# Dividing the merged attention heads earlier, in another loop, and handing them on through DRAM in token order

## The chip, the cores and the metric

The kernel runs on one core of a Trainium2 chip. The metric is the device time of one execution, in microseconds (us). TensorE (PE) multiplies matrices into PSUM; VectorE (DVE), ScalarE (ACT) and GpSimd (POOL) work on tiles in SBUF (DVE and ACT on PSUM too); SP, ACT and POOL also issue DMA transfers. Each engine has its own list of instructions, and they meet at semaphores.

## The reference

One layer of a decoder is computed for a prompt of 1024 tokens and 8 sample tokens with the same weights (1032 columns in all, `T`). The part that matters here:

```
h    = rms_norm(x, g_mix_pre)
q, k, v, c_b, u, g_a, g_c = project(h, w_in)
attn = merged heads of three dilated attention groups      # [1024, 512]: numerator / denominator
a    = attn @ w_attn_o                                     # 512 -> 1024
c    = (c_b * causal_conv(u)) @ w_conv_o                   # 1024 -> 1024
mix  = (sigmoid(g_a) * a + sigmoid(g_c) * c) @ w_o
x    = x + rms_norm(mix, g_mix_post)
x    = x + rms_norm(square(relu(rms_norm(x, g_ffn_pre) @ w_ff1)) @ w_ff2, g_ffn_post)
```

## The kernel before

All activations lie with channels on the 128 partitions and tokens along the row. The 1032 columns are taken in three chunks of 344 (`CH`). Every product is made of three matmuls, since each operand is split into a high part (a cast, `wh`, `hh`, `ah`) and the rest (a subtraction, `wl`, `hl`, `al`): high by high (L165), rest by high (L168), high by rest (L169). Weights come as tiles of 128x512 (`wr`), are split by ACT (L134) and by DVE or POOL (L135), and are held in at most seven pairs of buffers in the stages told of here.

`unit` computes one 128-row block of one projection for one chunk: 24 matmuls where the inner size is 1024, 12 where it is 512, all into one PSUM bank `ps_mm`. `bank` hands out four banks in turn, so a fifth chunk can begin only when the first has been read by whoever evacuates it.

The stages in question, in order:

- **Attention** writes, for each head, the unnormalised output `od_sum` to `num_d` in DRAM (L641) and the denominators to `den_d`. Within a row the tokens do not lie in order: they lie by class, that is by their remainder modulo 4, 256 tokens to a class. After it, the reciprocals of the denominators go to `rden_d` (L703), in the same order.
- **The convolution's projections**, which end with `cvh` and `cvl`.
- **The convolution's output projection** (`wco`, L933 to L951): for each of 8 row blocks `i`, three chunks of 24 matmuls on `cvh` and `cvl`; DVE multiplies each chunk out of PSUM with the sigmoid gate `sg[c]` into `m2` (L948; the tile is called m in the rows). For `i` under 4 the gate is loaded by POOL from `gc_d` (`gr`, L940) and ACT takes its sigmoid (L941); for the others PE computes the gate first. POOL stores each `m2` to `m2_d` (L950).
- **The attention output projection** (`wao`, L955 to L1015). When `cvh` and `cvl` are free, SP loads the numerators and the reciprocals, chunk by chunk and two of the four 128-row groups at a time, 86 tokens of a class at once (L972, L974): 36 transfers. Meanwhile PE computes the first attention gate (`g`, 72 matmuls). For each of six pieces DVE or POOL multiplies numerator by reciprocal (L981), and ACT and DVE split the product into `ah` and `al`, reading by class and writing in token order (L986, L987). Then PE alternates between two half units of the next gate and one chunk of the output projection: `run(ga, 2)`, `run(pa, 1)`, so 24 and 12 matmuls in turn.

Instructions that the code does not pin are placed on each engine by a scheduler, so the order on an engine is not always that of the lines. PE's order is that of the code.

Of the kernel before, what the change touches and what calls it, by code (L numbers as in the profile page):

```python
# [10 lines left out]
F32 = mybir.dt.float32  # L11
F32R = mybir.dt.float32r
AF = mybir.ActivationFunctionType
OP = mybir.AluOpType
# [4 lines left out]
P = 128  # L19
KT = 8  # L20
NQ = 1024
NB = 8
T = NQ + NB
CH = T // 3
# [3 lines left out]
def chunk(c):  # L28
    return slice(c * CH, (c + 1) * CH)
# [6 lines left out]
def tile_decoder_layer(  # L36
# [5 lines left out]
    nc = tc.nc  # L42

    const = ctx.enter_context(tc.tile_pool(name="const", bufs=1))
    dram = ctx.enter_context(tc.tile_pool(name="dram", bufs=1, space=DRAM))
# [16 lines left out]

    asm = const.tile([P, 4, NB], F32, name="asm")
    num_d = dram.tile([P, 4, NQ], F32, name="num_d")
    den_d = dram.tile([8, NQ], F32, name="den_d")
    rden_d = dram.tile([8, NQ], F32, name="rden_d")
    sq_d = dram.tile([NB, 3, 512], F32, name="sq_d")
# [103 lines left out]
    def whole(hi, lo):  # L171
        return lambda k, c: (hi[:, k, chunk(c)], lo[:, k, chunk(c)])
# [17 lines left out]
    def project(src, rhs, use):  # L190
        yield from several([(src, use)], rhs)
# [8 lines left out]
    def run(g, n=None):  # L200

        while n is None or n > 0:
            if next(g, run) is run:
                return
            n = n and n - 1
# [30 lines left out]
    def spread(ri):  # L236
        rb = bank(at, [P, 512], "ps_rb")
        for b, (o, w) in enumerate(NB3):
            pe(nc.tensor.transpose(rb[:, o:o + w], ri[:, b:b + 1].to_broadcast([P, P]), ident))  # L239
        return rb  # L240
# [37 lines left out]
    def copy_piece(n=1):  # L278
        for _ in range(n):
            if pieces:  # L280
                tc.keep_in_program_order(nc.scalar.dma_start(*pieces.pop(0)))


    with ExitStack() as st:
# [71 lines left out]
        with tc.tile_pool(name="xin", bufs=1) as xin:  # L356
# [26 lines left out]
            def apply(c, rb):  # L383
                return norm_apply(xin, x_sb[c], rb, 0, lambda k: hh[:, k:k + 2, chunk(c)],
                                  lambda k: hl[:, k:k + 2, chunk(c)],
                                  (nc.vector, nc.gpsimd) if c else (nc.vector,))
# [29 lines left out]
            a = apply(0, spread(ri))  # L416
# [11 lines left out]
            for c in range(3):  # L428
                run(g, 4)
                if c < 2:  # L430
                    ri = factors(sq)
                    run(g, 1)
                    a = apply(c + 1, spread(ri))
# [493 lines left out]
    def gate(pool, src, store):  # L927
        def use(c, ps):
            s = pool.tile([P, CH], F32, name="sg", tag="sg", bufs=4)
            nc.scalar.activation(s, ps, AF.Sigmoid)  # L930
            store[c] = s
        return project(src, h_in, use)

    lo_eng[:] = [nc.vector]
    with tc.tile_pool(name="sgc", bufs=1, side="right") as sgp:
        for i in range(KT):
            sg = {}
            if i < NRAW:
                gr = sgp.tile([P, T], F32, name="gr", tag="gr", bufs=2)
                nc.gpsimd.dma_start(gr, gc_d[i])  # L940
                nc.scalar.activation(gr, gr, AF.Sigmoid)  # L941
                sg = {c: gr[:, chunk(c)] for c in range(3)}
            else:
                run(gate(sgp, ("win", W1 + i), sg))
            m2 = sgp.tile([P, T], F32, name="m2", bufs=2)

            def use_cc(c, ps):
                nc.vector.tensor_tensor(m2[:, chunk(c)], ps, sg[c], op=OP.mult)  # L948
            run(project(("wco", i), whole(ch_, cl_), use_cc))
            nc.gpsimd.dma_start(m2_d[i], m2)  # L950
            copy_piece(1)  # L951
# [3 lines left out]
    with tc.tile_pool(name="apool", bufs=1) as apool:  # L955
        ah = apool.tile([P, 4, T], F32R, name="ah")
        al = apool.tile([P, 4, T], F32R, name="al")
        rv = rden_d.rearrange("(k a) t -> a k t", a=2)
        sgs = [{} for _ in range(KT)]
        with tc.tile_pool(name="pre", bufs=1) as pre:  # L960
            def by_class(t):
                return t.rearrange("p k (r j) -> p k r j", r=4)

            nums = []
            for c in range(3):
                w = min(NQ, CH * (c + 1)) - CH * c
                js = slice(CH // 4 * c, CH // 4 * c + w // 4)
                for k in (0, 2):
                    ks = slice(k, k + 2)
                    ar, rd = (pre.tile([P, 2, CH], F32, name=nm, bufs=6) for nm in ("num", "rden"))  # L970
                    for k1 in range(2):
                        nc.sync.dma_start(by_class(ar[:, :, 0:w])[:, k1], by_class(num_d[:, ks, :])[:, k1, :, js])  # L972
                        for a in range(2):
                            nc.sync.dma_start(by_class(rd[64 * a:64 * a + 64, :, 0:w])[:, k1],  # L974
                                              by_class(rv[a:a + 1, ks, :])[:, k1, :, js].to_broadcast([64, 4, w // 4]))
                    nums.append((c, ks, w, ar, rd))
            g = gate(apool, ("win", W1 + 8), sgs[0])
            for c, ks, w, ar, rd in nums:
                run(g, 1)
                s = slice(CH * c, CH * c + w)  # L980
                (nc.gpsimd if c else nc.vector).tensor_tensor(ar[:, :, 0:w], ar[:, :, 0:w], rd[:, :, 0:w], op=OP.mult)  # L981
                for k1 in range(2):
                    k = ks.start + k1
                    src = ar[:, k1, 0:w].rearrange("p (r j) -> p j r", r=4)
                    hi = ah[:, k, s].rearrange("p (j r) -> p j r", r=4)
                    nc.scalar.copy(hi, src)  # L986
                    nc.vector.tensor_tensor(al[:, k, s].rearrange("p (j r) -> p j r", r=4), src, hi.bitcast(F32),  # L987
                                            op=OP.subtract)
            nc.scalar.copy(ah[:, :, NQ:], asm)
            nc.vector.tensor_tensor(al[:, :, NQ:], asm, ah[:, :, NQ:].bitcast(F32), op=OP.subtract)  # L990
            run(g)
        mpool = m_stack.enter_context(tc.tile_pool(name="mpool", bufs=1, side="right"))
        mh = mpool.tile([P, KT, T], F32R, name="mh")
        ml = mpool.tile([P, KT, T], F32R, name="ml")

        def m2_tile():
            return apool.tile([P, CH], F32, name="m2c", tag="m2c", bufs=3)

        for i in range(KT):
            sg = sgs[i]  # L1000

            def use_a(c, ps):
                s = chunk(c)
                m2 = m2_tile()
                nc.gpsimd.dma_start(m2, m2_d[i, :, s])
                nc.vector.tensor_tensor(sg[c], ps, sg[c], op=OP.mult)
                nc.gpsimd.tensor_tensor(m2, m2, sg[c], op=OP.add)
                nc.scalar.copy(mh[:, i, s], m2)
                nc.vector.tensor_tensor(ml[:, i, s], m2, mh[:, i, s].bitcast(F32), op=OP.subtract)
            ga = gate(apool, ("win", W1 + 9 + i), sgs[i + 1]) if i + 1 < KT else iter(())  # L1010
            pa = project(("wao", i), whole(ah, al), use_a)
            for c in range(3):
                run(ga, 2)
                run(pa, 1)
            run(pa)  # L1015
            copy_piece(1)
# [320 lines left out]
```

## Time and profile before

| | us |
|---|---|
| median of 3 runs | 2048.09 (2047.76 to 2049.38) |
| the profiled execution's own time | 2052.08 |
| its span, first to last instruction | 2050.3 |
| PE busy with matmuls in the span | 1995.0 |
| DVE busy | 1056.0 |
| ACT busy | 687.2 |
| POOL busy | 512.7 |

The profile is of one execution, with the times of single instructions counted from the start of its span. PE is busy nearly all the time and its mean granted clock was 0.987 of full speed; so a gain can only come from a stretch in which PE waits or runs at a lower clock, and a loss from a new one.

### The profile page before, as it was taken

The numbers are of one execution on the slowest core, as the hardware profiler recorded it, in microseconds if no ns is written. First come the engines' busy times: TensorE is split into PE (matmuls) and PEld (weight loads), VectorE is DVE, ScalarE is ACT, GpSimd is POOL, SyncE is SP. The second block draws the span as 40 slices with busy tenths as digits, with TensorE's granted clock in tenths as the row PEclk, the third lists the DMA queues.
The fourth block names the chain that finished last, engine by engine and source line by source line (L and its number), as shares of the span: only waits on it lengthen the run. The fifth ranks groups of instructions, "written<-read, shape, count | busy, mean of one in ns | idle before, by whom it ended". The sixth has DMA issues, their size and how long they took to land. (4 is left out here: it accounts for less than half of the span.)

```text
span 2050.3 us, 31900 instructions
## 1 busy us (share of the span) xinstructions
PE 1995.0 (97%) x12877; PEld 1975.1 (96%) x12877; DVE 1056.0 (52%) x1829; ACT 687.2 (34%) x1351; POOL 512.7 (25%) x414
## 2 busy tenths in 40 slices
PE   7999999999999999999989999999999999999997
PEld 6999999999999999999989999899999999999996
DVE  7688668677653454642223321925554444444446
ACT  4365435544443222222113232543322222222233
POOL 3233413332333532520013232311211111111113
PEclk7999999999999999999999999999999999999998
DMA  4121222222324744435374441322221111111112
GB/s 145 53 71 38 87 68 66 58 87 89 107 67 151 227 160 162 156 134 198 114 169 130 140 155 33 96 93 84 98 88 43 52 45 49 42 47 57 42 32 83
DMA packets 89669, 195.52 MB, mean 95 GB/s; under 512 B 23489, under 2 KB 33857, under 8 KB 88625
## 3 DMA queue, kind: packets, MB, share of 16 engines
q1 hardware_dynamic: 78144, 116.97, 18.2%
q10 hardware_dynamic: 6672, 63.49, 9.3%
q0 software_dynamic: 4704, 13.01, 2.0%
q8 instruction: 101, 1.65, 0.3%
q14 instruction: 48, 0.39, 0.1%
HBM read 173.60 MB, written 74.29 MB: 121 GB/s over the span
## 5 line engine op out<-in xcount | busy, mean ns | idle before, releaser
L165 PE MATMUL ps_mm<-hh,wh 128*128 128x344 f32 x1824 | 594.2, 326 | 4.1 <-ACT sg L930 2.1
L168 PE MATMUL ps_mm<-hl,wh 128*128 128x344 f32 x1824 | 586.9, 322 | 3.7 <-DVE hl L248 1.9
L169 PE MATMUL ps_mm<-hh,wl 128*128 128x344 f32 x1824 | 586.3, 321 | 0.0
L135 POOL TENSOR_TENSOR wl<-wr,wh 128x512 fp32r<-128x512 f32 x177 | 235.4, 1331 | 867.5 <-ACT wh L134 827.2
L134 ACT CAST wh<-wr 128x512 fp32r<-128x512 f32 x320 | 195.3, 619 | 574.2 <-PE ps_mm L168 474.2
L165 PEld LDWEIGHTS ps_mm<-hh,wh 128*128 128x128 f32 x1824 | 346.6, 190 | 6.8 <-ACT hh L254 2.9
L168 PEld LDWEIGHTS ps_mm<-hl,wh 128*128 128x128 f32 x1824 | 346.1, 190 | 6.0 <-DVE hl L248 3.2
L169 PEld LDWEIGHTS ps_mm<-hh,wl 128*128 128x128 f32 x1824 | 346.1, 190 | 0.0
L165 PE MATMUL ps_mm<-gh,wh 128*128 128x344 f32 x768 | 246.2, 321 | 0.0
L165 PE MATMUL ps_mm<-rh,wh 128*128 128x344 f32 x768 | 245.9, 320 | 0.0
L169 PE MATMUL ps_mm<-rh,wl 128*128 128x344 f32 x768 | 245.8, 320 | 0.0
L169 PE MATMUL ps_mm<-gh,wl 128*128 128x344 f32 x768 | 245.4, 320 | 0.0
L168 PE MATMUL ps_mm<-gl,wh 128*128 128x344 f32 x768 | 245.4, 319 | 0.0
L168 PE MATMUL ps_mm<-rl,wh 128*128 128x344 f32 x768 | 245.0, 319 | 0.0
L1174 DVE TENSOR_TENSOR f<-ps_mm,f 128x344 f32<-128x344 f32 x336 | 167.2, 513 | 96.5 <-PE ps_mm L169 96.3
L1112 DVE TENSOR_TENSOR r<-r 128x344 f32<-128x344 f32 x96 | 59.6, 620 | 216.1 <-ACT rh L1111 216.0
L135 DVE TENSOR_TENSOR wl<-wr,wh 128x512 fp32r<-128x512 f32 x143 | 99.3, 698 | 128.2 <-ACT wh L134 128.0
L169 PEld LDWEIGHTS ps_mm<-gh,wl 128*128 128x128 f32 x768 | 144.7, 188 | 0.0
L168 PEld LDWEIGHTS ps_mm<-gl,wh 128*128 128x128 f32 x768 | 144.7, 188 | 0.0
L165 PEld LDWEIGHTS ps_mm<-gh,wh 128*128 128x128 f32 x768 | 144.7, 188 | 0.0
L165 PEld LDWEIGHTS ps_mm<-rh,wh 128*128 128x128 f32 x768 | 144.3, 188 | 0.0
L168 PEld LDWEIGHTS ps_mm<-rl,wh 128*128 128x128 f32 x768 | 144.3, 188 | 0.0
(255 smaller groups left out, 2935.2 us busy)
## 6 DMA issues: line engine op xcount, KB each, us to landing
wr<-in_win_dram SPq DMA_DIRECT2D x152, 256.0 KB, 2.9
wr<-in_wf_dram SPq DMA_DIRECT2D x128, 256.0 KB, 2.8
out_okv_dram<-in_cache_dram ACTq DMA_DIRECT2D x16, 1020.0 KB, 8.1
kt<-in_cache_dram SPq DMA_DIRECT2D x32, 256.0 KB, 3.4
x_sb<-in_xT_dram SPq DMA_DIRECT2D x12, 344.0 KB, 5.5
m_d<-m POOLq DMA_DIRECT2D x8, 516.0 KB, 7.8
m2c<-m_d POOLq DMA_DIRECT2D x24, 172.0 KB, 3.7
xk<-in_xT_dram SPq DMA_DIRECT2D x12, 344.0 KB, 4.1
```

What stands on the lines that cost most here:

```text
L134: pin_(nc.scalar.copy(hi, raw))
L135: pin_(eng.tensor_tensor(lo, raw, hi.bitcast(F32), op=OP.subtract))
L165: ins = nc.tensor.matmul(ps, wh, rh, start=(first and i == 0), stop=False)
L168: nc.tensor.matmul(ps, wh, rl, start=False, stop=False)
L169: nc.tensor.matmul(ps, wl, rh, start=False, stop=(last and i == n - 1))
L1112: pin(nc.vector.tensor_tensor(r, r, r, op=OP.mult))
L1174: pin(nc.vector.tensor_tensor(d, ps, d, op=OP.add))
```

## The change

The division moves out of the attention output projection. In the convolution's output projection, at row blocks 1 to 4, POOL loads one 128-row group of numerators (all 1024 tokens) and the two rows of reciprocals, each spread over 64 partitions; DVE multiplies them in one instruction that reads by class and writes in token order (`nat`), and POOL stores the result to a new array `nat_d`. Each of the three new tiles has one buffer. In the attention output projection SP then makes six contiguous loads from `nat_d` instead of 36, no product is left there, and ACT and DVE split pieces of 128x2x344 in six instructions each instead of twelve.

```
--- before.py
+++ after.py
@@ -62,6 +62,7 @@
     num_d = dram.tile([P, 4, NQ], F32, name="num_d")
+    nat_d = dram.tile([P, 4, NQ], F32, name="nat_d")
@@ -935,6 +936,16 @@
     with tc.tile_pool(name="sgc", bufs=1, side="right") as sgp:
         for i in range(KT):
             sg = {}
+            if 0 < i < 5:
+
+                j = i - 1
+                ar, rd, nat = (sgp.tile([P, NQ], F32, name=nm) for nm in ("num", "rden", "nat"))
+                nc.gpsimd.dma_start(ar, num_d[:, j, :])
+                for a in range(2):
+                    nc.gpsimd.dma_start(rd[64 * a:64 * a + 64, :], rden_d[2 * j + a:2 * j + a + 1, :].to_broadcast([64, NQ]))
+                ar4, rd4 = (t.rearrange("p (r j) -> p j r", r=4) for t in (ar, rd))
+                nc.vector.tensor_tensor(nat.rearrange("p (j r) -> p j r", r=4), ar4, rd4, op=OP.mult)
+                nc.gpsimd.dma_start(nat_d[:, j, :], nat)
@@ -955,37 +966,22 @@
-        rv = rden_d.rearrange("(k a) t -> a k t", a=2)
         sgs = [{} for _ in range(KT)]
         with tc.tile_pool(name="pre", bufs=1) as pre:
-            def by_class(t):
-                return t.rearrange("p k (r j) -> p k r j", r=4)
-
             nums = []
             for c in range(3):
                 w = min(NQ, CH * (c + 1)) - CH * c
-                js = slice(CH // 4 * c, CH // 4 * c + w // 4)
+                s = slice(CH * c, CH * c + w)
                 for k in (0, 2):
                     ks = slice(k, k + 2)
-                    ar, rd = (pre.tile([P, 2, CH], F32, name=nm, bufs=6) for nm in ("num", "rden"))
-                    for k1 in range(2):
-                        nc.sync.dma_start(by_class(ar[:, :, 0:w])[:, k1], by_class(num_d[:, ks, :])[:, k1, :, js])
-                        for a in range(2):
-                            nc.sync.dma_start(by_class(rd[64 * a:64 * a + 64, :, 0:w])[:, k1],
-                                              by_class(rv[a:a + 1, ks, :])[:, k1, :, js].to_broadcast([64, 4, w // 4]))
-                    nums.append((c, ks, w, ar, rd))
+                    ar = pre.tile([P, 2, CH], F32, name="numc", bufs=6)[:, :, 0:w]
+                    nc.sync.dma_start(ar, nat_d[:, ks, s])
+                    nums.append((ks, s, ar))
             g = gate(apool, ("win", W1 + 8), sgs[0])
-            for c, ks, w, ar, rd in nums:
+            for ks, s, ar in nums:
                 run(g, 1)
-                s = slice(CH * c, CH * c + w)
-                (nc.gpsimd if c else nc.vector).tensor_tensor(ar[:, :, 0:w], ar[:, :, 0:w], rd[:, :, 0:w], op=OP.mult)
-                for k1 in range(2):
-                    k = ks.start + k1
-                    src = ar[:, k1, 0:w].rearrange("p (r j) -> p j r", r=4)
-                    hi = ah[:, k, s].rearrange("p (j r) -> p j r", r=4)
-                    nc.scalar.copy(hi, src)
-                    nc.vector.tensor_tensor(al[:, k, s].rearrange("p (j r) -> p j r", r=4), src, hi.bitcast(F32),
-                                            op=OP.subtract)
+                nc.scalar.copy(ah[:, ks, s], ar)
+                nc.vector.tensor_tensor(al[:, ks, s], ar, ah[:, ks, s].bitcast(F32), op=OP.subtract)
```

PE's instructions and their order stay as they are. On the other engines the order moves at three places.

**DVE, where the convolution's output projection begins.** The rows are those from the last chunk of the convolution's own work (`yc`, `cvl`) to the first chunks of the output projection that are read out of PSUM (the tile `m2` of row block 0, then of row block 1). Before:

```order
L914 TENSOR_TENSOR yc<-ps_mm,yc 128x344
L864 COPY asm<-ps_sm 128x32
L916 TENSOR_TENSOR cvl<-yc,cvh 128x344
L948 TENSOR_TENSOR m_9518<-ps_mm,gr 128x344 x2
L135 TENSOR_TENSOR wl<-wr,wh 128x512 x2
L948 TENSOR_TENSOR m_9518<-ps_mm,gr 128x344
L948 TENSOR_TENSOR m_9614<-ps_mm,gr 128x344 x2
```

And after the change:

```order
L915 TENSOR_TENSOR yc<-ps_mm,yc 128x344
L865 COPY asm<-ps_sm 128x32
L917 TENSOR_TENSOR cvl<-yc,cvh 128x344
L947 TENSOR_TENSOR nat<-num,rden 128x1024 x4
L959 TENSOR_TENSOR m_9519<-ps_mm,gr 128x344 x2
L136 TENSOR_TENSOR wl<-wr,wh 128x512 x2
L959 TENSOR_TENSOR m_9519<-ps_mm,gr 128x344
L959 TENSOR_TENSOR m_9623<-ps_mm,gr 128x344 x2
```

All four new products stand ahead of the first chunk that is read out of PSUM, though the code writes them at row blocks 1 to 4.

**POOL, at the same place.** Its rows are DMA issues here: the gates `gr`, the stores of `m2`, and now the loads and stores of the division. Before:

```order
L940 DMA gr<-gc_d 128x1032 x2
L950 DMA m_d<-m_9518 128x1032
L940 DMA gr<-gc_d 128x1032
L950 DMA m_d<-m_9614 128x1032
L940 DMA gr<-gc_d 128x1032
```

And after (the three rows of the second division come twice more before the store of `m2`, and are left out):

```order
L951 DMA gr<-gc_d 128x1032
L943 DMA num<-num_d 128x1024
L945 DMA rden<-rden_d 64x1024 x2
L951 DMA gr<-gc_d 128x1032
L948 DMA nat_d<-nat 128x1024
L943 DMA num<-num_d 128x1024
L945 DMA rden<-rden_d 64x1024 x2
L948 DMA nat_d<-nat 128x1024
```

Each store of a quotient stands ahead of the loads for the next one, and all of them ahead of the first store of `m2` and of the third and fourth gate loads.

**SP, where the attention output projection begins.** Before, the first of the 36 loads, between weight loads:

```order
L126 DMA wr<-in_win_dram 128x512
L972 DMA num<-num_d 128x4x86
L974 DMA rden<-rden_d 64x4x86
L126 DMA wr<-in_win_dram 128x512
L974 DMA rden<-rden_d 64x4x86
L972 DMA num<-num_d 128x4x86
L974 DMA rden<-rden_d 64x4x86 x2
```

And after, all of the loads that are left:

```order
L127 DMA wr<-in_win_dram 128x512
L978 DMA numc<-nat_d 128x2x344 x2
L127 DMA wr<-in_win_dram 128x512
L978 DMA numc<-nat_d 128x2x344 x2
L978 DMA numc<-nat_d 128x2x336 x2
L127 DMA wr<-in_wao_dram 128x512
```

The place in SP's list is the same; what stands there is six transfers with rows of 344 tokens instead of 36 with rows of 86.

## Rows read from the trace of the kernel before

**Rows 1.** Windows over the attention output projection: length, busy us (instructions), clock, DMA share, GB/s.

```profile
core 0: us, PE busy (x) PEld busy (x) DVE busy (x) ACT busy (x) POOL busy (x), PEclk, DMA share, GB/s
1049.00:1060.00 11.00, 11.00 (x72) 11.00 (x71) 1.17 (x2) 0.48 (x1) 2.17 (x4) 1.00 0.96 285
1060.00:1070.00 10.00, 5.61 (x31) 5.09 (x30) 3.61 (x5) 3.28 (x5) 0.00 (x0) 0.92 1.15 184
1070.00:1080.00 10.00, 7.88 (x35) 7.60 (x34) 4.86 (x9) 4.68 (x9) 3.33 (x3) 0.74 0.85 166
1080.00:1090.00 10.00, 7.25 (x43) 6.60 (x42) 3.48 (x6) 4.41 (x7) 5.34 (x4) 0.94 0.26 73
1090.00:1100.00 10.00, 10.00 (x48) 10.00 (x49) 5.34 (x9) 3.36 (x7) 2.98 (x5) 0.72 0.50 185
1100.00:1150.00 50.00, 50.00 (x320) 50.00 (x319) 14.71 (x26) 13.43 (x27) 15.03 (x18) 1.00 0.47 150
```

**Rows 2.** Timeline of PE, 1048 to 1100: start, us, ..., [idle before <-releaser].

```profile
1048.77 0.32 PE L165 MATMUL ps_mm<-hh,wh 128*128 128x344 f32 x1
...
1066.13 0.42 PE L165 MATMUL ps_mm<-ah,wh 128*128 128x344 f32 x1 [2.10 <-ACT sg L930]
1068.84 0.66 PE L168 MATMUL ps_mm<-al,wh 128*128 128x344 f32 x1 [2.29 <-DVE al L987]
...
1074.26 0.43 PE L165 MATMUL ps_mm<-hh,wh 128*128 128x344 f32 x1 [2.12 <-ACT sg L930]
...
1089.06 0.66 PE L165 MATMUL ps_mm<-ah,wh 128*128 128x344 f32 x1 [2.62 <-ACT ah L986]
...
1099.01 0.33 PE L165 MATMUL ps_mm<-hh,wh 128*128 128x344 f32 x1
```

**Rows 3.** Timelines of DVE and POOL, 1058 to 1100: first products, and their waits.

```profile
1063.32 0.88 DVE L981 TENSOR_TENSOR num<-num,rden 128x688 f32<-128x688 f32 x1 [13.12 <-DMA rden<-rden_d]
...
1070.71 1.64 POOL L981 TENSOR_TENSOR num<-num,rden 128x688 f32<-128x688 f32 x1 [19.31 <-DMA rden<-rden_d]
```

**Rows 4.** DMA issues from 1045 to 1100: packets, then count, KB each, us to landing.

```profile
DMA packets 14313, 9.41 MB, mean 171 GB/s; under 512 B 13092, under 2 KB 13092, under 8 KB 14279
...
num<-num_d SPq DMA_DIRECT2D x8, 172.0 KB, 7.5
```

**Rows 5.** Timelines of PE, POOL and DVE where the convolution's output projection begins.

```profile
912.84 0.43 PE L165 MATMUL ps_mm<-cvh,wh 128*128 128x344 f32 x1
...
915.45 1.16 POOL L940 DMA_DIRECT2D gr<-gc_d  x2 [1.01 <-issue]
...
926.66 0.52 DVE L948 TENSOR_TENSOR m<-ps_mm,gr 128x344 f32<-128x344 f32 x1 [11.85 <-ACT gr L941]
```

**Rows 6.** Instructions by tile, POOL's loads of gr, then of m2c: us to landing.

```profile
DMA to landing us min/median/max: 5.3/8.4/9.2
...
DMA to landing us min/median/max: 2.5/3.7/8.5
```

**Rows 7.** POOL's timeline and DMA issues at 930 and 938: us to landing last.

```profile
929.53 0.54 POOL L950 DMA_DIRECT2D m_d<-m  x1 [12.92 <-DVE m L948]
930.05 0.54 POOL L940 DMA_DIRECT2D gr<-gc_d  x1
...
m_d<-m POOLq DMA_DIRECT2D x1, 516.0 KB, 4.8
gr<-gc_d POOLq DMA_DIRECT2D x1, 516.0 KB, 5.3
...
m_d<-m POOLq DMA_DIRECT2D x1, 516.0 KB, 7.6
gr<-gc_d POOLq DMA_DIRECT2D x1, 516.0 KB, 8.3
```

**Rows 8.** Durations by tile and by line: ns min/median/max, or busy us and mean ns.

```profile
L987 DVE TENSOR_TENSOR al<-num,ah x12: 723/752/804, 1068.1 to 1089.7; 128x344 fp32r<-128x344 f32 x8, 128x336 fp32r<-128x336 f32 x4
...
L1009 DVE TENSOR_TENSOR ml<-m2c,mh x24: 500/516/1235, 1092.2 to 1206.6; 128x344 fp32r<-128x344 f32 x24
...
L908 DVE SCALAR_TENSOR_TENSOR yc<-E,cwt,yc 128x1024 f32<-128x1024 f32 x1 | 1.3, 1285 | 0.0
```

## The prediction, as put on record before the run

> **What bounds the kernel now.** The page says that PE is busy for 1995 of 2050 us, so I looked only for what PE loses in the two stages that the diff touches: the attention output projection, from which work is taken, and the convolution's output projection, to which it is given. I read the windows first, then PE's timeline, then the timelines of those that PE waited for, and last the transfers.
>
> In the attention output projection the windows show the loss at once [rows 1]. From 1100 on, PE starts 320 matmuls in 50 us, 0.156 us each; between 1060 and 1100 it starts 157 in 40 us, where 256 would fit. The clock column falls to 0.74 and 0.72 in two of the windows: part of the loss is idle time, part is time at the lower of TensorE's two levels (1.2 and 2.4 GHz) after an idle time. PE's timeline names the waits [rows 2]: 2.10 for a sigmoid `sg`, 2.29 for `al`, 2.12 for `sg` again, 2.62 for `ah`. The `sg` that held PE stands behind casts to `ah` on ACT, so all four come from one place, the pieces that are divided and split. What made those late is in the timelines of DVE and POOL [rows 3]: the first product began at 1063.32 after DVE had waited 13.12 us for the reciprocals, and POOL's first at 1070.71 after 19.31 us. The DMA rows say why [rows 4]: 13092 of 14313 packets are under 512 B (86 tokens are 344 B), and a load of 172 KB took 7.5 us to land, though 172 KB of `m2c` lands in as little as 2.5 [rows 6].
>
> The loss by counting: from 1048.77, the first matmul of the first attention gate, to 1099.01, the first of the second chunk of the next gate but one [rows 2], the code has 72 + 3 x (24 + 12) + 24 + 12 = 216 matmuls. At 0.156 each they take 33.7 us; they took 50.2. **16.5 us is all that this stage can give back.**
>
> In the convolution's output projection PE does not wait now, but it comes near it. Its first matmul is at 912.84 and the first chunk is read out of PSUM at 926.66, because DVE waited 11.85 us for the sigmoid of the first gate [rows 5]. Four chunks of 24 matmuls fill the four banks in 15.0 us, so PE would stop at **927.8** if nothing had been read. The slack is half a microsecond.
>
> **What the change removes.** 36 loads on SP, two products on DVE and four on POOL, and the reading by class in the split (752 ns a piece against 516 where rows are read in order, [rows 8]). In their place stand six loads of 344 KB with rows of 1376 B. PE needs the first two at 1063.7 (gate of 72 matmuls and half units of 24 more, after 1048.77). The old loads, in the crowd that they made, took 7.5 at the median [rows 4]; even 10 us from 1049 leaves 4 us for two casts and two subtractions of under 1 us each. The third to sixth are needed 5.6 and 11 us later. So I take the whole 16.5 back, and as the other bound 8, if half of the four waits with their low clock stay. Behind the casts on ACT stand the sigmoids, and PE's banks wait for those; that is the way in which a remainder would show.
>
> **What it adds.** Here the order decides. On DVE the four new products stand in a row ahead of the first chunk that is read out of PSUM. Everything behind them waits: the chunks, hence PE's banks, hence PE; the weights' low parts; and on POOL the stores of `m2` and the third and fourth gate loads. And the four cannot overlap: each of their three tiles has one buffer, POOL's list has each store ahead of the next loads, and the next product may not write before that store has landed. One round is then: a store of 512 KB, a load of 512 KB and two loads of 256 KB, issued one after the other by POOL at 0.54 us each, until all have landed; then the product.
>
> *Transfers of a round.* The nearest rows are a store and a load of 516 KB that POOL issued together [rows 7]: the first pair (929.53 and 930.05) was down 5.8 us after its first issue, a second pair at 938, beside other copies, about 8.8. The bounds: from below, the last of four issues begins at 1.6 and lands no sooner than the 2.5 of a 172 KB load, 4.1 us. From above, the second pair plus 504 KB at its pace ((8.8 - 2.5)/860 KB), 12.5 us. I take the first pair plus 504 KB at its pace, 7.7 us, since with PE stopped few other transfers are started: weight loads and cache copies wait for PE too.
>
> *The product.* 1024 elements read in order took 1285 ns; one operand read by class costs 236 ns more per 344, so 0.70 us per 1024 [rows 8]. With one, none or two such operands at full price: 2.0, 1.3 or 2.7 us. I take 2.0 (the case measured).
>
> A round is 9.7 us, between 5.4 and 15.2. The first product's loads stand behind the first gate in POOL's list; two gate loads issued at 915.45 had landed by 925.2 at the latest (9.2 the longest, [rows 5, 6]), so the numerators by then, the reciprocals 1.9 later, and the first product ends at 929.1 (926.5 to 931.6). Three more rounds: **958.2** (942.7 to 977.2).
>
> *PE.* The first chunk is read 0.5 us after that; PE stood from 927.8 to 958.7, **30.9 us** (15.4 to 49.9). Then it starts at the low clock: after the wait of 2.62 us it started 48 matmuls in the window from 1090 to 1100 instead of 64 [rows 1], 16 x 0.156 = 2.5 us lost (I take that; 0 to 3). After that nothing is late again: the third gate is issued some 4 us after the last product and has landed and passed ACT within 11 more, while PE has two more chunks to compute and then four banks to fill, 22 us.
>
> The sum: 30.9 + 2.5 - 16.5 = **+16.9 us**. The profiled execution took 2052.08; the median of the runs is 4.0 lower, and I carry the difference over to it: 2048.1 + 16.9 = 2065.
>
> The Trainium skill has a price for these transfers of its own: "DMA: Bandwidth & Descriptors", section on the anatomy of one DMA on the gpsimd path, gives 2.0 us plus the bytes over 436 GB/s. By it, as an estimate, the 1536 KB of a round take 5.6 us, a round 7.6, and the kernel 2059; the pair of rows 7, which it puts at 4.4, took 5.8, so the trace bears it out only as a bound from below.
>
> **Rivals.**
> *Hidden after all (faster, 2032).* The products could end before PE runs out of banks, and all 16.5 would be kept. It begins to be a gain when PE stands for less than 14 us, that is when the last product ends by 941.3: a round of 4.1 us. Against it: POOL's issues and the shortest landing alone take 4.1, without the product. For it, only that no row shows a load that spreads one row over 64 partitions, and the reciprocals' part might cost nearly nothing.
> *Quick rounds (2046 to 2057).* Rounds of 5.5 to 7 us, since the stalled kernel leaves the DMA engines free. At 6.5: 927 + 19.5 = 946.5, a stall of 19.2, +5.2 us, 2053. Rows 7 speak against it: the quicker pair of only two thirds the bytes took 5.8.
> *Slow rounds (2073 to 2090).* Like the pair at 938, or because 64 partitions read the same 4 KB. At 13 us: the last product ends at 968, +27 us, 2075.
> *The gain does not come (2070 to 2076).* The stall as forecast, but the new loads meet the cache copy and the loads of `m2c` at 1049, where the DMA share was 0.96 [rows 1], and half of the old waits stay: +25 us, 2073.
>
> **How the numbers follow.** The forecast (rounds of 7 to 12 us, 2057 to 2073) has 55 in 100, quick rounds 15, slow rounds 17, the missing gain 8, hidden 5. The likeliest time is 2065. The range of 8 in 10 leaves out the hidden case, the quicker half of the quick rounds and the slowest of the slow ones: 2053 to 2080. A measurement of this kernel tells 0.2%, 4 us, from no change. Faster has the hidden case, 0.05; no change needs rounds of about 4 to 5.5 us, 0.05; slower has the rest, 0.90.
>
> **What would show it.** In the profile after: DVE idle between some 914 and 958 except for four products of about 2 us, each ended by a DMA; PE idle about 31 us from 928, released by the first chunk read out of PSUM; POOL's third gate load at about 962; a low clock just after; and no PE wait named `ah`, `al` or `sg` at the start of the attention output projection, with 216 matmuls there in about 34 us. I am wrong if the products stand further apart on the chip than in the list, with chunks between them, if a round takes 4 us, or if PE waits again at the casts to `ah`.

## The result, and the profile after

| | us |
|---|---|
| before, median of 4 runs | 2047.93 (2046.94 to 2049.38) |
| after, median of 4 runs | 2075.64 (2073.47 to 2079.85) |
| ratio | 1.0133, interval 1.0121 to 1.0144 |
| the profiled execution of after, and its span | 2075.51, 2073.7 |

The change makes the kernel 27.7 us slower. One thing has to be known for reading the traces: the convolution's output projection begins at 908.1 in the profiled execution of after and at 912.8 in that of before [rows 5], and between 908 and 914 in those of the experiments, though the work ahead of it is the same. So times are compared from the first matmul of this stage, and medians of four runs that lie 4 us apart are not told apart by themselves.

PE's waits from 900 to 1140 in the kernel after (us in total, times, longest). Before, there were four in this stretch, of 9.1 us in all, every one in the attention output projection [rows 2]:

```profile
PE ps_mm L166 <- DVE m L959: 39.5, 1, 39.5
```

PE's timeline after, at the start of the convolution's output projection, at that wait, at the start of the attention output projection, and at its 217th matmul (start, us):

```profile
908.13 0.43 PE L166 MATMUL ps_mm<-cvh,wh 128*128 128x344 f32 x1
...
963.03 0.65 PE L166 MATMUL ps_mm<-cvh,wh 128*128 128x344 f32 x1 [39.53 <-DVE m L959]
...
1086.30 0.32 PE L166 MATMUL ps_mm<-hh,wh 128*128 128x344 f32 x1
...
1120.27 0.33 PE L166 MATMUL ps_mm<-hh,wh 128*128 128x344 f32 x1
```

The stage that was given the work lasts 1086.30 - 908.13 = 178.2 us; before it lasted 1048.77 - 912.84 = 135.9 [rows 2, 5]. It loses 42.2: 39.5 of waiting, 2.7 after it. The stage from which the work was taken lasts 1120.27 - 1086.30 = 34.0 us instead of 50.2, and gains 16.3. Together that is +25.9. What comes behind the 216 matmuls took 953.4 us instead of 951.3; over all the runs told of here, with a stall or without one, it lies between 951.3 and 954.4, so these 2 us are not shown to come from the change.

Windows of after, behind the wait and over the attention output projection (columns as in [rows 1]):

```profile
960.00:965.00 5.00, 1.97 (x7) 1.97 (x8) 4.48 (x7) 0.00 (x0) 0.56 (x1) 0.50 0.22 84
965.00:970.00 5.00, 5.00 (x24) 5.00 (x23) 0.89 (x3) 0.00 (x0) 1.06 (x2) 0.65 0.95 305
970.00:975.00 5.00, 5.00 (x33) 5.00 (x33) 1.89 (x4) 2.31 (x3) 0.00 (x0) 1.00 0.61 202
1086.00:1096.00 10.00, 10.00 (x65) 10.00 (x65) 1.21 (x2) 0.62 (x1) 2.14 (x4) 1.00 0.90 289
1096.00:1106.00 10.00, 10.00 (x66) 10.00 (x65) 6.77 (x10) 6.84 (x13) 0.14 (x1) 1.00 0.64 217
```

PE comes back at the granted clock 0.50 (the 1.2 GHz level, after 39.5 us without a matmul), starts 24 matmuls in 5 us at 0.65 and 33 at 1.00. The attention output projection now runs at full clock without a gap. Where before 157 matmuls fitted into 40 us [rows 1], there are 65 or 66 in each 10.

ACT's and PE's timelines after: the first cast of a loaded piece, and the first matmuls on it.

```profile
1096.73 0.77 ACT L983 CAST ah<-numc 128x688 fp32r<-128x688 f32 x1 [9.72 <-DMA numc<-nat_d]
...
1101.40 0.32 PE L166 MATMUL ps_mm<-ah,wh 128*128 128x344 f32 x1
1101.55 0.32 PE L169 MATMUL ps_mm<-al,wh 128*128 128x344 f32 x1
```

The first of the new loads took 10.2 us to land, more than the old ones at their median [rows 4], and still its cast is done 3.9 us before PE comes to it.

DVE's timeline after, where PE stands, with what ended the idle time before each product:

```profile
925.52 2.03 DVE L947 TENSOR_TENSOR nat<-num,rden 128x1024 f32<-128x1024 f32 x1 [15.42 <-DMA gr<-gc_d]
936.96 2.04 DVE L947 TENSOR_TENSOR nat<-num,rden 128x1024 f32<-128x1024 f32 x1 [9.42 <-DMA rden<-rden_d]
948.80 2.04 DVE L947 TENSOR_TENSOR nat<-num,rden 128x1024 f32<-128x1024 f32 x1 [9.80 <-DMA rden<-rden_d]
960.52 2.03 DVE L947 TENSOR_TENSOR nat<-num,rden 128x1024 f32<-128x1024 f32 x1 [9.68 <-DMA rden<-rden_d]
962.47 0.92 DVE L959 TENSOR_TENSOR m<-ps_mm,gr 128x344 f32<-128x344 f32 x2
```

The view names a gate load for the first product, which reads no gate; its last reciprocals, issued at 912.4, landed 12.6 us later, at 925.0. Four products, 11.4 to 11.8 us from one to the next, and right behind the last one the first chunk that DVE reads out of PSUM; PE starts 0.6 us after that. POOL's timeline shows a round from the other side, a store and the next three loads as soon as a product is done:

```profile
939.29 0.56 POOL L948 DMA_DIRECT2D nat_d<-nat  x1 [9.37 <-DVE nat L947]
939.85 0.53 POOL L943 DMA_DIRECT2D num<-num_d  x1
940.37 1.03 POOL L945 DMA_DIRECT2D rden<-rden_d  x2
```

Then to landing, by tile: num, rden, nat_d (us, min/median/max; the longest are the first round's).

```profile
DMA to landing us min/median/max: 7.0/7.3/11.7
...
DMA to landing us min/median/max: 7.2/7.5/12.6
...
DMA to landing us min/median/max: 3.0/3.0/3.2
```

And what moved in that round: windows of after from the store's issue on (the last two columns are the DMA share and GB/s).

```profile
939.00:940.50 1.50, 0.00 (x0) 0.00 (x0) 0.00 (x0) 0.00 (x0) 1.21 (x3) 0.50 0.07 27
...
940.50:941.50 1.00, 0.00 (x0) 0.00 (x0) 0.00 (x0) 0.00 (x0) 0.90 (x2) 0.50 1.03 406
941.50:942.50 1.00, 0.00 (x0) 0.00 (x0) 0.00 (x0) 0.00 (x0) 0.00 (x0) 0.50 0.66 160
942.50:943.50 1.00, 0.00 (x0) 0.00 (x0) 0.00 (x0) 0.00 (x0) 0.00 (x0) 0.50 0.99 156
943.50:944.50 1.00, 0.00 (x0) 0.00 (x0) 0.00 (x0) 0.00 (x0) 0.00 (x0) 0.50 0.83 254
944.50:945.50 1.00, 0.00 (x0) 0.00 (x0) 0.00 (x0) 0.00 (x0) 0.00 (x0) 0.50 1.07 270
945.50:946.50 1.00, 0.00 (x0) 0.00 (x0) 0.00 (x0) 0.00 (x0) 0.00 (x0) 0.50 0.78 176
946.50:947.50 1.00, 0.00 (x0) 0.00 (x0) 0.00 (x0) 0.00 (x0) 0.00 (x0) 0.50 0.36 102
```

About 1 us passes before the first byte. The store goes through in little more than 1 us at 406 GB/s; the loads need 6 us for twice its bytes; and 1.3 us after the last of these windows the next product starts, at 948.80. The loads are the round.

### The profile page after: what moved, and what is told of

Read it like the earlier page. It is cut to its first block, busy times and chain, and to the rows that moved or that the text cites. A ratio compares the mean times of both kernels' runs of the same rounds, so it can differ in the third digit from the quotient of the medians.

```text
span 2073.7 us, 31865 instructions
## 1 busy us (share of the span) xinstructions
PE 1987.7 (96%) x12877; PEld 1969.1 (95%) x12877; DVE 1058.6 (51%) x1825; ACT 682.6 (33%) x1345; POOL 513.6 (25%) x426
## 5 line engine op out<-in xcount | busy, mean ns | idle before, releaser
L170 PEld LDWEIGHTS ps_mm<-rh,wl 128*128 128x128 f32 x768 | 144.7, 188 | 0.0
```

The source lines that it names most:

```text
L170: nc.tensor.matmul(ps, wl, rh, start=False, stop=(last and i == n - 1))
```

## The experiments

Most are edits of the kernel after; the run with the division unused and the last two are built on the kernel before. The length of a stage is counted from its first matmul to the first of the next stage, as above. Where a run leaves part of the computation out, its expectation says which.

### Was it the place in DVE's list?

**Code order.** The product and the reading of a chunk out of PSUM are kept in the order of the code on DVE:

```
-                nc.vector.tensor_tensor(nat.rearrange("p (j r) -> p j r", r=4), ar4, rd4, op=OP.mult)
+                pin(nc.vector.tensor_tensor(nat.rearrange("p (j r) -> p j r", r=4), ar4, rd4, op=OP.mult))
...
-                nc.vector.tensor_tensor(m2[:, chunk(c)], ps, sg[c], op=OP.mult)
+                pin(nc.vector.tensor_tensor(m2[:, chunk(c)], ps, sg[c], op=OP.mult))
```

> The changed kernel with two pins: DVE takes the products of the division and the chunks read out of PSUM in the order of the code, so one product stands behind each of the first four row blocks and never four in a row. Tiles, transfers and PE are as in the changed kernel. Theory (the order on DVE makes the loss: four products, each behind a round of transfers, hold the first chunk): PE no longer waits in the convolution's output projection, since a round of some 11.7 us now runs beside a row block of 11.3 us of PE work, and the 16.3 us of the attention output projection stay: 2048 - 16 = 2032 us. Rival (the added transfers themselves, 6 MB on POOL's queue, and the later gates and stores make the loss, wherever the products stand): still above 2060 us, with PE waits in that stage.

Measured: 2036.29 (2035.0 to 2039.29), ratio 0.9941 [0.992, 0.9961], faster than before. One wait of PE for DVE is left in the stage. DVE's timeline shows where it comes from, the third and fourth product:

```profile
PE ps_mm L166 <- DVE m L959: 1.9, 1, 1.9
```

```profile
956.73 2.39 DVE L947 TENSOR_TENSOR nat<-num,rden 128x1024 f32<-128x1024 f32 x1 [10.25 <-DMA rden<-rden_d]
...
972.49 2.36 DVE L947 TENSOR_TENSOR nat<-num,rden 128x1024 f32<-128x1024 f32 x1 [10.87 <-DMA rden<-rden_d]
```

The order on DVE was the cause: nearly all of the stall is gone, with the same transfers. POOL's list changes with it, since a store of `m2` can now be issued between two rounds, but POOL did not hold the first chunk in the kernel after: its gate was ready at 922.2, and DVE stood from 910.1 to 925.5. ACT's timeline of after:

```profile
921.13 1.07 ACT L952 ACTIVATE gr<-gr 128x1032 f32<-128x1032 f32 x1
```

In code order a row block takes 11.3 us, and with PE running the loads share the DMA engines with weights, gates, stores and cache copies: the DMA share from 930 to 960 was 0.99, where the run without the division, below, has 0.72, and the products came 13.5 to 16.3 us apart. DVE stood for 10 us at the last two, and the stage lasted 139.6 us, 3.7 more than without the division: 1.9 of waiting and 1.8 behind it.

**Late blocks.** As in code order, and the products at row blocks 4 to 7, in which PE computes the gate too:

```
-            if 0 < i < 5:
+            if 3 < i:
...
-                j = i - 1
+                j = i - 4
```

> The four products keep the order of the code on DVE, as in the run in code order, and stand in row blocks 4 to 7, in which PE computes the gate too, so that 22.6 us lie between them instead of 11.3. Theory (what was still lost in code order, 3.8 us in the convolution's output projection, is products that come late for their loads): no wait of PE for DVE in that stage, all of the 16 us kept, median 2032. Rival (the added transfers and products cost some us there wherever they stand): 2036 as in code order.

Measured: 2036.31 (2033.75 to 2039.07), ratio 0.994 [0.9925, 0.9955]. The profile bears out the theory: PE waits for nothing from 905 to 1130, the stage lasts 135.9 us as before the change, and no product waits:

```profile
955.71 2.45 DVE L947 TENSOR_TENSOR nat<-num,rden 128x1024 f32<-128x1024 f32 x1
...
1023.67 2.24 DVE L947 TENSOR_TENSOR nat<-num,rden 128x1024 f32<-128x1024 f32 x1
```

The median does not show it: two of its four runs are at 2034 and two at 2039, so it can't be told from code order by time. What is shown is that the stage is whole again, not that the kernel is faster than with code order.

**Late in the code only.** The same two lines, without the pins.

> The division is written at row blocks 4 to 7, as in the run with late blocks, but DVE's order is left to the scheduler. Theory (the place in DVE's list decides, and the scheduler puts the four products ahead of the first chunk from there too): PE stands for some 39 to 41 us and the median is 2074 to 2078, as in the changed kernel. Rival (the later place in the code is enough): 2032 to 2037, as with late blocks kept in code order.

Measured: 2077.81 (2076.24 to 2080.8), ratio 1.0137 [1.0122, 1.0153]; PE stood 43.1 us at the same place, and the four products stood 11.4 to 11.6 us apart from 931.36 on. Where the code writes the division has no say while the scheduler puts it at the head of DVE's list.

### The two halves of the change

**No division.** The block of the division is left out, and the six loads read `num_d`:

```
-            if 0 < i < 5:
-                ...
-                nc.gpsimd.dma_start(nat_d[:, j, :], nat)
...
-                    nc.sync.dma_start(ar, nat_d[:, ks, s])
+                    nc.sync.dma_start(ar, num_d[:, ks, s])
```

> The changed attention output projection alone: the block of the division in the convolution's output projection is left out, and the six contiguous loads read the numerators as attention left them. Left out of the computation: the division by the denominators and the token order. Theory (the two halves of the change are independent, a gain of 16.3 us and a loss of 42): 2048 - 16 = 2032 us, no PE wait for ah, al or sg, and none in the convolution's output projection. Rival (the gain is smaller, since the new loads collide with other transfers): above 2038 us.

Measured: 2032.55 (2031.13 to 2035.28), ratio 0.9922 [0.9902, 0.9942], with no wait for sg, ah or al: 15.6 us less than before, which is the term of the gain.

**Division unused.** The division as in after, and the attention output projection as in the kernel before.

> The other half alone: the kernel before, with the new division block added in the convolution's output projection and its result stored but not read; the attention output projection divides for itself as before. Nothing is left out. Theory (loss of 39.5 us of wait and 2.7 at the low clock, gain of nothing): 2048 + 42 = 2090 us. Rival (part of the stall is given back later because the stall leaves the transfers time to finish): below 2082 us.

Measured: 2095.32 (2091.62 to 2097.43), ratio 1.023 [1.0206, 1.0255]; PE's wait for DVE was 39.2 us, as in after. The loss stands alone, without the gain. It came out some 5 us above the expectation. The profiled execution, at 2091.62 the fastest of the four, does not show why: the stage with the division lasted 177.1 us, and the 216 matmuls of the attention output projection took 49.5, no more than before, though PE's waits there lie otherwise (7.1 us for `sg`, 3.2 for `al`, 0.3 for `ah`). The excess of the median stays open.

### What makes a round so long?

**Loads ahead.** SP issues the loads, into two buffers each; the quotient keeps one:

```
-                ar, rd, nat = (sgp.tile([P, NQ], F32, name=nm) for nm in ("num", "rden", "nat"))
-                nc.gpsimd.dma_start(ar, num_d[:, j, :])
+                ar, rd, nat = (sgp.tile([P, NQ], F32, name=nm, bufs=1 if nm == "nat" else 2) for nm in ("num", "rden", "nat"))
+                nc.sync.dma_start(ar, num_d[:, j, :])
```

(and the reciprocals likewise)

> The changed kernel, four products still in a row ahead of the first chunk, but the loads of the division go by SP, not POOL, and into two buffers each, so that the loads for the next product run while one waits; only the store of one quotient is still between two products. Theory (the loss is four rounds one after the other, and each round is mostly its loads): the rounds shrink to the pace of the transfers, 1 MB in 5 to 7 us; the last product ends about 30 us after the first matmul of the stage instead of 54.4, PE waits some 15 us instead of 39.5, and the time is 2045 to 2056 us. Rival (a round is long because of POOL's store and the landing, not the loads): rounds stay near 10 us, PE waits 33 us or more, 2068 us or more.

Measured: 2066.78 (2065.55 to 2069.56), ratio 1.0089 [1.0069, 1.011]; PE's wait 31.2 us. Neither theory held as it stood. The products were at 924.64, 939.12, 948.23 and 953.53, the last three released by the store of the quotient ahead of them, so rounds of 14.5, 9.1 and 5.3 us. Two buffers take the loads out of the round where they have already landed, as in the last one. In the first round the store, issued at 927.02, took 12.0 us to land: the next loads (from 926.75) and two cache copies of 1020 KB (issued at 926.80 and 928.01) passed at the same time. No cache copy was issued during a round of the kernel after, so this run does not price the loads by itself.

**No spread.** Each load of a row of reciprocals, spread over 64 partitions, becomes a load of 64 rows of numerators:

```
-                    nc.gpsimd.dma_start(rd[64 * a:64 * a + 64, :], rden_d[2 * j + a:2 * j + a + 1, :].to_broadcast([64, NQ]))
+                    nc.gpsimd.dma_start(rd[64 * a:64 * a + 64, :], num_d[64 * a:64 * a + 64, (j + 1) % 4, :])
```

> Like the changed kernel, but the two loads of reciprocals of each division read 64 different rows of the numerators instead of one row spread over 64 partitions; the number, size and order of the transfers are the same, and the quotients become products of numerators. Theory (the spread rows are what makes a round slow): a round falls from 11.7 us towards the 9.7 forecast, PE stands for some 33 us instead of 39.5, median about 2068. Rival (any 1536 KB that POOL issues in such a round take this long): rounds stay at 11.4 to 11.8 us, PE's wait at 39 to 40, median 2075.

Measured: 2075.7 (2073.65 to 2080.4), ratio 1.0136 [1.012, 1.0151]; rounds of 11.2 to 11.3 us, PE's wait 38.4. My theory falls: the spread costs 0.2 to 0.6 us a round, 0.4 at the mean.

**Numerators only**, and **reciprocals only**: the loads of the one or the other are left out, and the product has one operand twice.

```
-                for a in range(2):
-                    nc.gpsimd.dma_start(rd[64 * a:64 * a + 64, :], rden_d[2 * j + a:2 * j + a + 1, :].to_broadcast([64, NQ]))
```

> Like the changed kernel, but without the loads of reciprocals (the numerators are multiplied by themselves): a round is a store and a load of 512 KB and the product. Theory (spread rows are slow): a round takes about 8 us or less, since a store and a load of this size were down 5.8 us after the first issue in the kernel before; PE stands for 28 us at most, median 2060 to 2064. Rival (the bytes alone count): two thirds of 9.6 us and the product, 8.4 us; PE stands for some 29 us, 2065. By itself this run can't tell them apart, beside the run with the reciprocals alone it can.

```
-                nc.gpsimd.dma_start(ar, num_d[:, j, :])
```

> Like the changed kernel, but without the loads of numerators (the reciprocals are multiplied by themselves): a round is a store of 512 KB, two spread loads of 256 KB and the product, the same bytes as in the run with the numerators alone. Theory (spread rows are slow): rounds of 10 us or more, PE stands for 34 us or more, median at least 2070. Rival (the bytes alone count): the same rounds as with the numerators alone, some 8.4 us, PE's wait 29 us, 2065.

Measured: 2061.01 (2060.3 to 2066.08), ratio 1.0069 [1.0052, 1.0086], PE's wait 25.9, and 2068.2 (2065.93 to 2069.7), ratio 1.0095 [1.008, 1.011], PE's wait 28.9. DVE's timelines, the last two products of each; numerators only:

```profile
940.07 2.03 DVE L945 TENSOR_TENSOR nat<-num 128x1024 f32<-128x1024 f32 x1 [6.14 <-DMA num<-num_d]
948.30 2.02 DVE L945 TENSOR_TENSOR nat<-num 128x1024 f32<-128x1024 f32 x1 [6.20 <-DMA num<-num_d]
```

Reciprocals only:

```profile
946.00 2.03 DVE L946 TENSOR_TENSOR nat<-rden 128x1024 f32<-128x1024 f32 x1 [6.23 <-DMA rden<-rden_d]
955.14 2.04 DVE L946 TENSOR_TENSOR nat<-rden 128x1024 f32<-128x1024 f32 x1 [7.11 <-DMA rden<-rden_d]
```

Rounds of 8.2 to 9.3 us in the one and 8.3 to 9.1 in the other, for two thirds of the bytes: the bytes count, whatever rows they come from, and whether one load or two bring them. From 8.3 to 11.7, the third 512 KB of a round costs about 3.4 us. The 7 us between the two medians are not the rounds alone: PE's waits differ by 3.0 in the profiled executions, and the stage begins 3.9 us later in the second (913.4, not 909.5).

**Loads by SP.** As after, single buffers too, but SP issues the loads:

```
-                nc.gpsimd.dma_start(ar, num_d[:, j, :])
+                nc.sync.dma_start(ar, num_d[:, j, :])
```

(and the reciprocals likewise)

> Like the changed kernel, single buffers and all, but SP issues the loads of numerators and reciprocals instead of POOL; the store of the quotient stays with POOL. Theory (the bytes of a round pass at some 155 GB/s only through the queue that POOL feeds): rounds of 9 us or less, PE stands for 31 us at most, median 2067 or less. Rival (they take as long through either queue): rounds of 11 us or more, PE stands for 38 us or more, 2074 to 2077.

Measured: 2071.39 (2070.15 to 2075.43), ratio 1.0112 [1.0098, 1.0126]; PE's wait 35.3. Rounds of 10.9, 11.9 and 10.7 us: wait and median lie between theory and rival, the rounds nearly where the rival has them. A cache copy of 1020 KB was issued as each of the first two began (922.43 and 933.62), none in the last. At 10.7 without one, POOL's queue explains some 1 us of a round and no more. The 4.2 us less of waiting are 2.6 of an earlier first product (its end 16.8 us after the stage's first matmul, not 19.4) and 1.6 of rounds.

### What made the pieces late before the change?

**Numerators by class.** On the run without the division, the attention output projection takes the undivided numerators in the old way:

```
-                    nc.sync.dma_start(ar, num_d[:, ks, s])
+                    for k1 in range(2):
+                        nc.sync.dma_start(by_class(ar[:, :, 0:w])[:, k1], by_class(num_d[:, ks, :])[:, k1, :, js])
```

(and the split as in the kernel before)

> No division anywhere; the attention output projection loads the undivided numerators in the old way, by class, 12 loads with rows of 344 B, and splits them by class in twelve instructions each as before; the 24 loads of reciprocals and the six products are left out. Theory (what held PE in that stage was the crowd of loads and the products behind it, so with a third of the loads and no product the pieces are there in time): no waits for sg, ah or al beyond 1 to 2 us, median 2032 to 2036, as with the division left out and contiguous loads. Rival (short rows and the split by class are what costs): half of the waits stay, 2040 or more.

**Loads, no product.** The same with the 24 loads of reciprocals (L974 of the kernel before) between them, read by nobody.

> Like the run with the numerators by class, but the 24 loads of reciprocals stand where the kernel before has them; nothing reads them, and the six products are left out. The numerators' loads stand between them in SP's list. Theory (the crowd of 36 loads is what made the pieces late): at least half of the waits at sg, ah and al and of their low clock come back, 2040 or more. Rival (the wait of the six products for both loads, and their own time, made them late): the numerators alone are there in time, no wait beyond 2 us, 2032 to 2036.

Measured: 2033.7 (2031.35 to 2035.66), ratio 0.9924 [0.9912, 0.9937], no PE wait at all from 900 to 1140; and 2041.4 (2038.47 to 2045.21), ratio 0.9962 [0.9949, 0.9975], with these:

```profile
PE ps_mm L166 <- ACT sg L931: 2.7, 1, 2.7
PE ps_mm L166 <- ACT ah L986: 0.4, 1, 0.4
PE ps_mm L169 <- DVE al L987: 0.4, 1, 0.4
```

Loads by class cost nothing here as long as there are twelve, short rows and all. With all 36 in SP's list the numerators are issued from 1046.1 to 1073.8 instead of 1046.9 to 1061.1, the last cast to `ah` starts at 1077.2 instead of 1067.5, and half of the gain is lost. In the kernel before, behind the products, the last subtraction, which follows that cast, starts at 1089.7 [rows 8]. (The stage's first matmul is at 1046.0, 1046.7 and 1048.8 in the three.) Its 216 matmuls take 34.0 us with the twelve loads, 41.0 with all 36, and 50.2 with the products too: taken out in this order, the loads of reciprocals and the products cost about half each. No run has the products without the crowd. The theory of the crowd was right for one half of the loss only.

## Why the prediction came out as it did

It said slower, by a stall in the convolution's output projection larger than what the other stage gives back. That is what happened, and the time came out 10.6 us above the likeliest, inside the range. The forecast's rounds of 7 to 12 us held, but its own time, 2057 to 2073, was missed by 2.6 us; the range held because it took in most of the slow-round rival. Its steps:

**The gain**, 16.5 us, "the whole": 16.3 measured, and the run without the division gives it alone. Right. The reason behind it was half right: the short rows, which the DMA rows [rows 4] suggested, are not the price by themselves. It is the 24 loads of reciprocals in SP's list and the products behind them.

**Four products ahead of the first chunk, unable to overlap**: right. Code order removes nearly the whole stall, late blocks all of it, and the same late place in the code without the pins brings it back.

**When PE runs out of banks**, 15.0 us after its first matmul: it stopped at 963.03 - 39.53 = 923.50, 15.4 after. Right.

**The product**, 2.0 us: 2.03. The number is right, the case behind it in part luck: 2.0 was the price with one operand read by class, and here both are; at full price for both it would have been 2.7. The second costs nothing to be seen here.

**The transfers of a round**, 7.7 us: 9.1 to 9.5 from the store's issue to the next product, and 0.3 more from the product's end to that issue. This term was mis-sized, and with it the three rounds: 35.0 us instead of 29.1, 5.9 more. The step was "I take the first pair plus 504 KB at its pace", a pace from which I had first taken off a load of 172 KB and its 2.5 us. The run with the numerators alone is that pair here: 5.9 us from the store's issue to the product in its last two rounds (942.39 to 948.30 the last), so its 5.8 was right. The third 512 KB cost not 1.9 but about 3.4; in proportion to the bytes the pair would have given 5.8 x 1536 / 1032 = 8.6 for all three. Of the reasons that the slow-round rival gave, 64 partitions reading the same 4 KB is refuted by the run without the spread.

**The first product** ends 16.3 us after the stage's first matmul: 19.4. Also mis-sized, by 3.1. Its loads landed after up to 12.6 us, beside two gate loads, a weight load and cache copies; I had given them 1.9 us more than the gates. With SP issuing them it was 16.8.

**The low clock after the stall**, 2.5 us: 2.7. Right.

So 30.9 became 30.9 + 5.9 + 3.1 - 0.4 (the later stop) = 39.5 us. With 2.7 and -16.3 that is +25.9, where +27.7 was measured between the medians. The time itself lies where the slow-round rival put it, with rounds of 11.7 us instead of its 13 and a later first product. The rival of the missing gain is refuted (no wait for `ah`, `al` or `sg`), and so are quick rounds (none under 11.4 us) and the hidden case.

The Trainium skill's page "DMA: Bandwidth & Descriptors", section on the anatomy of one DMA on the gpsimd path, gives 2.0 us plus the bytes over 436 GB/s. For the store of 512 KB that is 3.2 us as an estimate, and the trace agrees: 3.0. For a round it gave 7.6 with the product, and the trace has 11.7: the loads behind the store do not follow it here.

## What to carry to other kernels

Work moved into a stage "that has time" is put where the scheduler sets it on each engine, not where the code writes it: look at what then stands behind its longest wait, and keep the order by hand if that is the instruction that frees PE's banks. In a chain of single buffers, store, load and product add up, so price a round by a measured transfer of the same kind and scale it by its bytes at least (8.6 us here, where 9.1 to 9.5 were measured); taking a short transfer and its time off first, as I did, made it shorter still (7.7). A place where the slots are longer than a loaded round (22.6 us here against 13.5 to 16.3) hides what a place with 11.3 us does not.

## What the runs showed of the hardware

The loads of a round ran at 102 to 270 GB/s while the DMA share stood mostly between 0.66 and 1.07, in a kernel whose store had just passed at 406. In the same execution the loads of `numc`, also from DRAM to SBUF, ran faster. In this window all that moved, 1.41 MB, went through SP's queue and was almost all `numc`; the last of the four us is its tail:

```profile
1097.00:1101.00 4.00, 4.00 (x27) 4.00 (x27) 2.14 (x3) 2.81 (x6) 0.00 (x0) 1.00 0.98 352
```

So loads as such are not limited to that rate, nor does POOL's queue explain it (a round with SP's loads took 10.7 us), nor the spread rows. Here several loads were under way at once, with rows of 1376 B and not of 4 KB; which of these matters no run shows, so what slows the few loads of a round stays open. The low clock cost 2.7 us after a wait of 39.5 us and about 2.5 after one of 2.62 [rows 1, 2]: between these two its price did not grow with the wait.
